# First layer of a hybrid decoder trunk: part of GpSimd's elementwise work is given to VectorE, and the whole program is put in a new order

## The chip, the core and the metric

The kernel runs on one core of a Trainium2 chip. The metric is the device time of that core in microseconds (us). In the profile TensorE is PE (its weight load is PEld), VectorE is DVE, ScalarE is ACT, GpSimd is POOL and SyncE is SP.

## The reference, cut to what matters

Two decoder layers on 512 tokens of width 1024, all in float32. The change touches the first half of the first layer: one input projection, whose columns feed a pooling mixer, an indexer that picks 128 keys for each query, and attention over the picked keys with a partial rotary embedding.

```
h = rmsnorm(x, ln_mix[0]);  p = h @ w_in_ab
u_pool, q, k, v, qi, ki, wi = columns of p
q, k, qi, ki = partial_rope(...)            # ki after its own rmsnorm
y_a = pool_mixer(u_pool)                    # 4 groups, causal windows 2, 4, 8, 16
s_idx = sum_h relu(qi_h . ki) * wi_h;  sel = top_k(s_idx, 128)      # causal
y_b = softmax(q . k[sel] / 8) @ v[sel]      # 4 blocks of 128 queries
x = x + [y_a, y_b] @ w_out_ab
x = x + swiglu(rmsnorm(x));  then layer 1 (gated linear recurrence, swiglu) and a final rmsnorm
```

`partial_rope` turns pairs of the first 16 of each 64 columns: `x1*cos - x2*sin`, `x2*cos + x1*sin`.

## The kernel before

Activations lie transposed, 128 channels by 512 tokens. Each fp32 operand of a projection is kept as a high part and a low part, and each product is three matmuls: high by high (`BH,wh`), low of the activation by high of the weight (`BL,wh`), and high by low of the weight (`BH,wl`). A weight unit of up to 512 columns arrives by DMA in `raw`, ScalarE rounds it to `wh` (a ring of 6 buffers), and a subtraction on VectorE or GpSimd makes `wl` (`split`, lines 490 to 497). Which engine subtracts is set by `lo_eng[0]`, a function of the running number u of the unit.

Work of the first layer in the order in which it is written: units 0 to 5 project the indexer's queries (two slabs), 6 and 7 its key, 8 and 9 the attention's key, 10 and 11 its value, 12 to 19 four slabs of queries, 20 to 27 the four groups of the pooling mixer. `rope` is called eight times (two indexer queries, the indexer's key, the attention's key, four slabs of queries): a shuffle of rows on VectorE, a product with the cosine on VectorE, a product with the sine, and a sum. The mixer adds shifted copies of a page on GpSimd (1, 2, 3 and 4 additions for the four groups). `topk` finds, for query blocks 3, 2 and 1, the threshold of the 128 largest scores by 16 rounds of MAX and MATCH_REPLACE on VectorE (512, 384 and 256 keys wide), and ends with one comparison that makes a bf16 mask; TensorE adds that mask to the scores by a matmul with the identity (`bk<-pa,idb`). Units 28 to 35 are the mixer's output projection (`w_oa`, all low parts on GpSimd); its results are added to `xT` on VectorE, and the two PSUM banks that it uses come free by these additions.

The order in which each engine executes is not the order of the code. `Plan` records every operation with its dependences, gives each an estimated duration, and runs a list scheduler forward and backward six times; then for each row (seed, sigma, a, w) of the table `MOVES` it disturbs the priorities of the operations that start between a and a+w (in ns of its own estimate) by random numbers, plans three times more, and keeps the order with the least estimated end. The instructions are then issued in that order from one line, so nearly every row of the profile says L414 (`getattr(self.real[o.eng], o.call)`), and instructions are told apart by tiles. Each engine executes its own list strictly in that order.

Names: `bk` PSUM banks, `pa` and `pg` pages of 128x512 in SBUF, `sm` small tiles, `BH`/`BL` the high and low parts of the activation (later also of the mixer's and the attention's output), `xT` the residual stream, `trib`/`idb` bf16 tiles of the causal mask and the identity.

Of the kernel before, what the change touches and what calls it, by code (L numbers as in the profile page):

```python
# [40 lines left out]
ITERS = 6  # L41

MOVES = (
# [20 lines left out]
)  # L64
PAGES = 38
RPAGES = 20
# [351 lines left out]
def trunk(ctx: ExitStack, tc: tile.TileContext, xt, xp, pos, vecs, ident, dup, tri, lmask, invc, select,  # L418
          w_ab, w_kw, w_pool, w_oa, w_ob, w_c, w_oc, w_gu, w_dn, w_dq, out):
    nc = Plan(tc)  # L420
# [3 lines left out]
    def new(shape, dt, name):  # L424
        t = cp.tile(shape, dt, name=name)
        return t[tuple(slice(None) for _ in shape)]
# [60 lines left out]
    lo_eng = [lambda u: nc.vector]  # L487
# [21 lines left out]
    def units(src, sizes, cols=P):  # L509
        t = load(src)  # L510
        off = 0
        for s in sizes:
            yield split(t[:, off:off + s * cols], cols)
            off += s * cols
# [159 lines left out]
    class Stage:  # L674
# [12 lines left out]
        def next(self):  # L687
            n = 1 + 2 * (self.n % 2)
            self.n += 1
            return self.b[0], self.b[n], self.b[n + 1]  # L690
# [152 lines left out]
    def std(srcs, ah, al):  # L843

        ps = main.get()
        us = [(src, s) for src, s in srcs]
        n, tot = 0, sum(len(k) for _, s in us for k in s)
        for src, s in us:
            for u, ks in zip(units(src, [len(k) for k in s]), s):
                mm3(ps, u, ah, al, ks, n == 0, n + len(ks) == tot)  # L850
                n += len(ks)
        return ps
# [4 lines left out]
    def layer0(br):  # L857
# [3 lines left out]
        trib = new([P, H2], BF16, "trib")  # L861
        upm = new([P, P], I32, "upm")
        neg = new([P, P], F32, "neg")
        lo_eng[0] = lambda u: nc.gpsimd if u % 4 < 3 else nc.vector


        nc.sync.dma_start(vec, vecs)
# [7 lines left out]
        ps = side.get()  # L875
# [4 lines left out]
        for j in range(KD):  # L880
# [4 lines left out]
            if j in (0, 1, 4):  # L885
                k0, k1 = {0: (0, 1), 1: (1, 4), 4: (4, 8)}[j]
                for q in range(2):
                    u = next(units(w_ab[10 + q][:, P * k0:P * k1], [k1 - k0]))
# [56 lines left out]
        for src, dst in ((CE, Ct), (SE, St)):  # L945
            ps = side.get()
# [12 lines left out]
        pages.put(acc)  # L959
        nc.vector.tensor_mul(r2, r_, r_)  # L960

        def rope(dst, src, c, s, slow=False):
            sh = pages.get()
            nc.vector.stream_shuffle(sh, src, SH)
            nc.vector.tensor_mul(dst, src, c)
            nc.gpsimd.tensor_mul(sh, sh, s)
            (nc.gpsimd if slow else nc.vector).tensor_add(dst, dst, sh)
            pages.put(sh)


# [4 lines left out]
        main.put(kps)  # L975
        qi = [pages.get() for _ in range(2)]
        rope(qi[0], pq[0], Ct, St)
        main.put(pq[0])
        ss = col_sums([ksq], 64)
# [16 lines left out]
        side.put(rkp)  # L996
        ki = pages.get()
        rope(ki, kin, Ct, St)
        rope(qi[1], pq[1], Ct, St)
        main.put(pq[1])  # L1000
        rp = bcast(r_)
        R, RC, RS = pages.get(), pages.get(), pages.get()
# [36 lines left out]
        def scores(at):  # L1039
            for b, w in ((3, 2), (2, 9), (1, 9)):  # L1040
                if w == at:
                    x = index(b)
                    sc[b] = x, topk(b, x)
# [5 lines left out]
        ps = std([(w_ab[8], two8)], xh, xl)  # L1049
# [4 lines left out]
        ps = std([(w_ab[9], two8)], xh, xl)  # L1054
# [11 lines left out]
        qT = []  # L1066
        for j in range(4):
            scores(3 + j)
            ps = std([(w_ab[4 + j], two8)], xh, xl)
            qT.append(pages.get())  # L1070
            rope(qT[j], ps, RC, RS, True)
            main.put(ps)

        def attend(b, bias, ops):
# [74 lines left out]
        for g in range(2):  # L1149
            for x, y in zip(khl, kd2[2 * g:]):  # L1150
                ps = side.get()
# [4 lines left out]
        for j in range(4):  # L1156
# [7 lines left out]
            ps = side.get()  # L1164
# [49 lines left out]
        for z in range(2):  # L1214
            ts = slice(z * H2, z * H2 + H2)
            for n, (m, u) in enumerate(held):
                ps = main.get()
# [319 lines left out]

    r0, r1, r2 = Bridge(V_FFN), Bridge(V_MIX + 8), Bridge(V_FFN + 8)
    layer0(r0)
    pages.free = [b for b in pages.free if all(b is not x for x in early_pg)]  # L1540
    ffn(0, r1)
# [98 lines left out]
```

## Time and profile before

| | us |
|---|---|
| median of 3 runs | 1209.56 (1207.65 to 1212.93) |
| the profiled execution | 1210.61 |
| its span, first to last instruction | 1208.8 |
| PE busy | 1171.1 (97%) |
| DVE busy | 977.6 (81%) |
| ACT busy | 754.6 (62%) |
| POOL busy | 231.3 (19%) |

The profiled execution is 1.8 us longer than its span, and 1.05 us above the median. PE's busy share counts pipelined matmuls, so a short wait of PE shows as idle time only where it is longer than what is still in flight.

### The profile page before, as it was taken

How to read it: one execution, taken by the hardware profiler on the slowest of the kernel's cores; microseconds unless marked ns; L12 is line 12 of the kernel's file. 1: busy time of each engine (PE TensorE's matmuls, PEld its weight loads, DVE VectorE, ACT ScalarE, POOL GpSimd, SP SyncE). 2: the span in 40 equal slices, each digit the busy share in tenths (PEclk: the TensorE clock that was granted, in tenths of full speed). 3: DMA queues.
4: the chain of work that ended last, by engine and by line, in shares of the span. 5: the costliest groups of instructions: out<-in, count | busy, mean ns of one | idle time of the engine just before them, and what ended most of it. 6: DMA issues, size and time to landing. Idle time of an engine off the chain costs nothing.

```text
span 1208.8 us, 23135 instructions
## 1 busy us (share of the span) xinstructions
PE 1171.1 (97%) x8563; PEld 1074.0 (89%) x8563; DVE 977.6 (81%) x2116; ACT 754.6 (62%) x1753; POOL 231.3 (19%) x209
## 2 busy tenths in 40 slices
PE   8997999999999999998999999999999999999996
PEld 6775658999999988998899999988999999998996
DVE  7799965997777794777999999976987777894676
ACT  6336974766666672655777767744776666672563
POOL 4465112121111000113322222111221111000111
PEclk9998999999999999998999999999999999999999
DMA  9212023589867534576675444316489876634652
GB/s 330 85 53 70 18 53 87 170 232 235 230 173 208 129 115 139 135 169 175 209 180 138 125 121 109 100 57 158 159 235 233 227 185 174 161 103 123 150 151 70
DMA packets 72369, 180.60 MB, mean 149 GB/s; under 512 B 6144, under 2 KB 20544, under 8 KB 72256
## 3 DMA queue, kind: packets, MB, share of 16 engines
q1 hardware_dynamic: 51584, 141.37, 36.0%
q0 software_dynamic: 20672, 37.75, 18.7%
q8 instruction: 67, 1.10, 0.4%
q14 instruction: 46, 0.38, 0.1%
HBM read 177.00 MB, written 2.10 MB: 148 GB/s over the span
## 4 chain that ended last, share of the span: by engine, by line
PE 71%; DVE 7%; DMA 5%; ACT 4%; issue 2%; POOL 1%; DVEq 0%; POOLq 0%; ACTq 0%
PE bk L414 71%; DVE wl L414 3%; DMA raw<-in_w_dq 2%; DMA raw<-in_w_gu 2%; DVE pg L414 2%; ACT wh L414 2%; ACT pg L414 1%; POOL pg L414 1%; DVE raw L414 1%; DVE BL L414 1%; ACT bk L414 1%; DVE xT L414 1%; DMA raw<-in_w_c 0%; DVE pa L414 0%; DVE sm L414 0%
## 5 line engine op out<-in xcount | busy, mean ns | idle before, releaser
L414 PE MATMUL bk<-BH,wh 128*128 128x256 f32 (+1 forms) x2088 | 587.0, 297 | 9.9 <-ACT bk L414 3.9
L414 PE MATMUL bk<-BL,wh 128*128 128x256 f32 (+1 forms) x2088 | 588.5, 294 | 3.4 <-DVE BL L414 2.1
L414 PE MATMUL bk<-BH,wl 128*128 128x256 f32 (+1 forms) x2088 | 579.1, 294 | 1.7 <-DVE wl L414 1.3
L414 ACT ACTIVATE wh<-raw 128x512 fp32r<-128x512 f32 (+2 forms) x644 | 378.8, 603 | 280.2 <-PE bk L414 236.6
L414 DVE TENSOR_TENSOR wl<-raw,wh 128x512 fp32r<-128x512 f32 (+1 forms) x609 | 399.1, 672 | 111.5 <-ACT wh L414 92.6
L414 PEld LDWEIGHTS bk<-BH,wh 128*128 128x128 f32 x2088 | 389.8, 192 | 25.7 <-ACT bk L414 7.3
L414 PEld LDWEIGHTS bk<-BL,wh 128*128 128x128 f32 x2088 | 393.5, 192 | 13.3 <-DVE BL L414 3.5
L414 PEld LDWEIGHTS bk<-BH,wl 128*128 128x128 f32 x2088 | 388.6, 192 | 10.8 <-DVE wl L414 2.2
L414 PE MATMUL bk<-pr,wh 128*128 128x256 f32 (+1 forms) x784 | 190.4, 331 | 0.5 <-ACT wh L414 0.5
L414 PEld LDWEIGHTS bk<-pr,wh 128*128 128x128 f32 x784 | 132.0, 189 | 15.3 <-ACT wh L414 0.7
L414 PE MATMUL bk<-pr,wl 128*128 128x256 f32 (+1 forms) x392 | 129.0, 332 | 0.6 <-DVE wl L414 0.6
L414 DVE TENSOR_TENSOR raw<-raw 128x512 f32<-128x512 f32 (+1 forms) x152 | 102.7, 680 | 10.7 <-DMA raw<-in_w_gu 5.5
L414 POOL DMA_DIRECT2D raw<-in_w_gu x44 | 48.0, 1090 | 328.5 <-DMA raw<-in_w_gu 124.3
L414 DVE TENSOR_TENSOR pg<-pg,pg 128x256 f32<-128x256 f32 (+2 forms) x203 | 99.2, 499 | 9.0 <-ACT pg L414 4.5
L414 ACT COPY pg<-bk 128x256 f32<-128x256 f32 (+6 forms) x212 | 76.2, 365 | 29.4 <-PE bk L414 26.4
L414 ACT COPY bk<-bk 128x256 f32<-128x256 f32 x222 | 77.5, 362 | 23.9 <-PE bk L414 23.5
L414 PEld LDWEIGHTS bk<-pr,wl 128*128 128x128 f32 x392 | 73.5, 188 | 8.1 <-DVE wl L414 1.1
L414 PE MATMUL bk<-pg,pg 128*128 128x128 f32 (+3 forms) x578 | 66.7, 259 | 2.7 <-issue 1.6
L414 POOL TENSOR_TENSOR wl<-raw,wh 128x512 fp32r<-128x512 f32 (+3 forms) x35 | 45.8, 1313 | 93.6 <-ACT wh L414 85.7
L414 PEld LDWEIGHTS bk<-pg,pg 128*128 128x128 f32 (+3 forms) x578 | 55.3, 167 | 9.0 <-issue 2.8
L414 POOL TENSOR_TENSOR pg<-pg,pg 128x256 f32<-128x256 f32 (+1 forms) x36 | 39.3, 1094 | 114.3 <-ACT pg L414 62.5
L414 POOL DMA_DIRECT2D raw<-in_w_dq x16 | 17.5, 1096 | 223.2 <-DVE wl L414 164.1
(167 smaller groups left out, 1062.8 us busy)
## 6 DMA issues: line engine op xcount, KB each, us to landing
raw<-in_w_gu SPq DMA_DIRECT2D x44, 768.0 KB, 5.6
raw<-in_w_gu SPq DMA_DIRECT2D x64, 512.0 KB, 5.0
raw<-in_w_gu POOLq DMA_DIRECT2D x44, 512.0 KB, 6.6
raw<-in_w_c SPq DMA_DIRECT2D x16, 768.0 KB, 5.3
raw<-in_w_c SPq DMA_DIRECT2D x21, 512.0 KB, 3.9
raw<-in_w_dq SPq DMA_DIRECT2D x16, 576.0 KB, 5.7
raw<-in_w_c POOLq DMA_DIRECT2D x16, 512.0 KB, 6.9
raw<-in_w_dn SPq DMA_DIRECT2D x16, 448.0 KB, 3.4
```

Of the source, the lines that this page charges most:

```text
L414: getattr(self.real[o.eng], o.call)(*map(_real, o.args), **{k: _real(v) for k, v in o.kw.items()})
```

## The change

Three edits in `layer0`, and another table `MOVES` (75 rows in place of 60):

- units 0 to 27: GpSimd subtracts for odd u alone (14 of 28), in place of u % 4 < 3 (21 of 28). VectorE gets units 0, 2, 4, ..., and gives 3, 7, 11, ... to GpSimd;
- the product with the sine of all eight rotations goes from GpSimd to VectorE;
- the sum of the four rotations of the query slabs goes from GpSimd to VectorE.

```
@@ -41,26 +41,30 @@
 MOVES = (
-    (353236198, 1000, 372111, 20000), (664781755, 200, 1057486, 200000), (787263731, 2000, 158073, 40000),
...
+    (288545018, 1000, 132344, 40000), (1047664193, 50, 817488, 80000), (4522707, 2000, 934044, 40000),
...
@@ -861,7 +865,7 @@
-        lo_eng[0] = lambda u: nc.gpsimd if u % 4 < 3 else nc.vector
+        lo_eng[0] = lambda u: nc.gpsimd if u % 2 else nc.vector
@@ -959,12 +963,12 @@
-        def rope(dst, src, c, s, slow=False):
+        def rope(dst, src, c, s):
             sh = pages.get()
             nc.vector.stream_shuffle(sh, src, SH)
             nc.vector.tensor_mul(dst, src, c)
-            nc.gpsimd.tensor_mul(sh, sh, s)
-            (nc.gpsimd if slow else nc.vector).tensor_add(dst, dst, sh)
+            nc.vector.tensor_mul(sh, sh, s)
+            nc.vector.tensor_add(dst, dst, sh)
             pages.put(sh)
@@ -1068,7 +1072,7 @@
-            rope(qT[j], ps, RC, RS, True)
+            rope(qT[j], ps, RC, RS)
```

Since the planner starts from other operations and other random numbers, the lists of all engines differ from end to end. Three places follow.

POOL, in the middle of the input projections. `wl` rows are low parts; the others are products and sums of rotations. Before:

```order
L414 TENSOR_TENSOR pa6_111<-pa6_111,pg14_139 128x512
L414 TENSOR_TENSOR pa10_115<-pa10_115,pg14_139 128x512
L414 TENSOR_TENSOR pa16_121<-pa16_121,pa13_118 128x512
L414 TENSOR_TENSOR wl4_94<-raw2_83,wh4_88 128x512
L414 TENSOR_TENSOR wl5_95<-raw2_83,wh5_89 128x512
L414 TENSOR_TENSOR wl0_90<-raw0_81,wh0_84 128x512
L414 TENSOR_TENSOR pa9_114<-pa9_114,pg14_139 128x512
L414 TENSOR_TENSOR pg7_132<-pg7_132,pa13_118 128x512
L414 TENSOR_TENSOR pg6_131<-pg6_131,pg7_132 128x512
L414 TENSOR_TENSOR wl2_92<-raw1_82,wh2_86 128x512
L414 TENSOR_TENSOR wl3_93<-raw1_82,wh3_87 128x512
L414 TENSOR_TENSOR pg9_134<-pg9_134,pa13_118 128x512
```

The same place on POOL with the change, up to the first addition of the mixer (`128x511`):

```order
L418 TENSOR_TENSOR wl5_95<-raw2_83,wh5_89 128x512
L418 TENSOR_TENSOR wl1_91<-raw0_81,wh1_85 128x512
L418 TENSOR_TENSOR wl3_93<-raw1_82,wh3_87 128x512
L418 TENSOR_TENSOR wl5_95<-raw2_83,wh5_89 128x512
L418 TENSOR_TENSOR wl1_91<-raw0_81,wh1_85 128x512
L418 TENSOR_TENSOR wl3_93<-raw1_82,wh3_87 128x512
L418 TENSOR_TENSOR wl5_95<-raw2_83,wh5_89 128x512
L418 TENSOR_TENSOR wl1_91<-raw0_81,wh1_85 128x512
L418 TENSOR_TENSOR wl3_93<-raw1_82,wh3_87 128x512
L418 TENSOR_TENSOR pg9_134<-pg5_130 128x511
```

The rotations have left POOL, and every second low part; POOL's whole list has 194 rows in place of 213.

DVE, from the first MAX of query block 3 on (`pa18`, `pa19` hold the 512-wide scores). Before:

```order
L414 MAX sm2_98<-pa18_123 128x8
L414 TENSOR_TENSOR pg8_133<-bk0_143,pa12_117 128x512
L414 MATCH_REPLACE pa19_124<-sm2_98,pa18_123 128x512
L414 MAX sm3_99<-pa19_124 128x8
L414 MATCH_REPLACE pa18_123<-sm3_99,pa19_124 128x512
L414 MAX sm4_100<-pa18_123 128x8
L414 MATCH_REPLACE pa19_124<-sm4_100,pa18_123 128x512
L414 STREAM_SHUFFLE pg11_136<-bk1_144 128x512
L414 MAX sm5_101<-pa19_124 128x8
L414 TENSOR_TENSOR pg10_135<-bk1_144,pa12_117 128x512
L414 MATCH_REPLACE pa18_123<-sm5_101,pa19_124 128x512
L414 TENSOR_TENSOR wl5_95<-raw2_83,wh5_89 128x512
```

The same place on DVE with the change:

```order
L418 MAX sm2_98<-pa18_123 128x8
L418 STREAM_SHUFFLE pg7_132<-bk2_145 128x512
L418 MATCH_REPLACE pa19_124<-sm2_98,pa18_123 128x512
L418 TENSOR_TENSOR pg6_131<-bk2_145,pa12_117 128x512
L418 MAX sm3_99<-pa19_124 128x8
L418 TENSOR_TENSOR pg7_132<-pg7_132,pa13_118 128x512
L418 MATCH_REPLACE pa18_123<-sm3_99,pa19_124 128x512
L418 TENSOR_TENSOR pg6_131<-pg6_131,pg7_132 128x512
L418 MAX sm4_100<-pa18_123 128x8
L418 TENSOR_TENSOR wl2_92<-raw1_82,wh2_86 128x512
L418 MATCH_REPLACE pa19_124<-sm4_100,pa18_123 128x512
L418 TENSOR_TENSOR pg8_133<-bk0_143,pa12_117 128x512
```

Between two rounds of the selection there now stand rotations and low parts. From the first MAX to the comparison that ends block 3, DVE's list has 113 rows in place of 94, and it holds 4 MAX of block 2 in place of 6.

PE, at the end of the input projections (`bk1<-..wl3` is the last of them): the mixer's four small products (`pa6` holds the four pool weights, a pair of rows each), the doubling of the attention's key (`pa4`), and the first unit of `w_oa` (`wh4_88`, `wl4_94`). Before:

```order
L414 MATMUL bk1_144<-BH3_76,wl3_93 128x512
L414 MATMUL bk6_149<-pg7_132,pa6_111 128x256 x2
L414 MATMUL bk7_150<-pg2_127,pa6_111 128x256 x2
L414 MATMUL bk5_148<-pg13_138,pa6_111 128x256 x2
L414 MATMUL bk7_150<-BH0_73,pa4_109 128x512
L414 MATMUL bk7_150<-BL0_77,pa4_109 128x512
L414 MATMUL bk6_149<-pg17_142,pa6_111 128x256 x2
L414 MATMUL bk5_148<-BL0_77,pa4_109 128x512
L414 MATMUL bk7_150<-BL2_79,pa4_109 128x512
```

The same place on PE with the change:

```order
L418 MATMUL bk7_150<-BL2_79,pa4_109 128x512
L418 MATMUL bk2_145<-pa0_105,BH2_75 128x256
L418 MATMUL bk7_150<-BH0_73,wh4_88 128x512
L418 MATMUL bk7_150<-BL0_77,wh4_88 128x512
L418 MATMUL bk7_150<-BH0_73,wl4_94 128x512
L418 MATMUL bk5_148<-pg13_138,pa6_111 128x256 x2
L418 MATMUL bk7_150<-BH1_74,wh4_88 128x512
L418 MATMUL bk7_150<-BL1_78,wh4_88 128x512
L418 MATMUL bk6_149<-pg17_142,pa6_111 128x256 x2
L418 MATMUL bk7_150<-BH1_74,wl4_94 128x512
```

Five matmuls of `w_oa` now stand ahead of the last mixer product (`pg17`), where before there was none; up to the first matmul with the mask of block 3 there are 41 of them in place of 35.

## Rows read from the trace of the kernel before

**Rows 1.** Windows by stage: busy us (x instructions) of each engine, granted clock, DMA share, GB/s.
```profile
0.00:60.00 60.00, 53.87 (x259) 39.87 (x260) 45.98 (x104) 30.98 (x61) 28.74 (x28) 0.97 0.60 208
60.00:125.00 65.00, 57.59 (x240) 42.73 (x238) 62.50 (x126) 31.47 (x66) 38.23 (x30) 0.95 0.19 59
100.00:125.00 25.00, 17.59 (x68) 11.74 (x66) 23.45 (x46) 16.78 (x36) 11.44 (x10) 0.86 0.07 22
...
125.00:210.00 85.00, 84.20 (x427) 57.10 (x427) 60.97 (x195) 58.45 (x155) 12.01 (x11) 1.00 0.21 51
540.00:810.00 270.00, 262.91 (x2199) 250.15 (x2198) 246.98 (x586) 187.62 (x489) 64.53 (x57) 0.98 0.50 136
810.00:1208.00 398.00, 384.38 (x2908) 367.20 (x2906) 299.83 (x602) 237.02 (x525) 48.02 (x47) 0.99 0.61 162
```
**Rows 2.** Waits of PE from 100 to 130 us: us in total, times, longest.
```profile
PE bk L414 <- DVE pg L414: 4.7, 3, 2.9
...
PE bk L414 <- DVE xT L414: 1.1, 1, 1.1
```
**Rows 3.** Chain of work that ended last, first layer: start, us, what.
```profile
109.46 0.76 DVE pg L414 x2
...
124.89 0.68 DVE xT L414
...
125.61 69.72 PE bk L414 x314
```
**Rows 4.** Groups on POOL by shape, 0 to 60 us, then 60 to 125: busy, mean ns.
```profile
L414 POOL TENSOR_TENSOR wl<-raw,wh 128x512 fp32r<-128x512 f32 x11 | 15.5, 1419 | 16.2 <-ACT wh L414 14.8 <-DMA xT<-in_xp 1.4
...
L414 POOL TENSOR_TENSOR pg<-pg,pg 128x512 f32<-128x512 f32 x3 | 3.9, 1294 | 0.2
```
**Rows 5.** Groups on DVE by shape, 300 to 500 us, where POOL hardly works.
```profile
L414 DVE TENSOR_TENSOR wl<-raw,wh 128x512 fp32r<-128x512 f32 x101 | 67.8, 687 | 28.6 <-ACT wh L414 20.6 <-PE bk L414 6.9
```
**Rows 6.** Groups on DVE by shape, 0 to 60 us.
```profile
L414 DVE TENSOR_TENSOR pg<-pg,pg 128x512 f32<-128x512 f32 x7 | 8.4, 1206 | 0.1
...
L414 DVE SCALAR_TENSOR_TENSOR sm<-sm 128x4 f32<-128x4 f32 x12 | 3.5, 295 | 0.2
L414 DVE TENSOR_TENSOR wl<-raw,wh 128x512 fp32r<-128x512 f32 x3 | 3.1, 1040 | 0.0
L414 DVE TENSOR_TENSOR pa<-pa,pa 128x512 f32<-128x512 f32 x3 | 3.1, 1036 | 0.0
...
L414 DVE TENSOR_TENSOR sm<-sm 128x4 f32<-128x4 f32 x6 | 0.9, 157 | 0.1
```
**Rows 7.** Groups on DVE by shape, 60 to 125 us.
```profile
L414 DVE TENSOR_TENSOR pg<-bk,pa 128x512 f32<-128x512 f32 x6 | 4.1, 676 | 0.5 <-PE bk L414 0.5
...
L414 DVE MAX8 sm<-pa 128x8 f32<-128x384 f32 x7 | 3.9, 560 | 0.2
L414 DVE MATCH_REPLACE8 pa<-sm,pa 128x384 f32<-128x384 f32 x6 | 3.3, 546 | 0.0
L414 DVE TENSOR_TENSOR wl<-raw,wh 128x512 fp32r<-128x512 f32 x2 | 3.0, 1514 | 0.0
...
L414 DVE SCALAR_TENSOR_TENSOR pa<-pg,tok,pa 128x512 f32<-128x512 f32 x2 | 2.3, 1168 | 0.2
...
L414 DVE TENSOR_TENSOR pg<-pg,pg 128x16 f32<-128x16 f32 x7 | 2.2, 328 | 0.0
```
**Rows 8.** Timeline of POOL, then of DVE: start, us, instruction.
```profile
70.56 1.30 POOL L414 TENSOR_TENSOR pg<-pg,pg 128x512 f32<-128x512 f32 x1
...
70.86 1.55 DVE L414 TENSOR_TENSOR wl<-raw,wh 128x512 fp32r<-128x512 f32 x1
...
122.80 1.50 DVE L414 TENSOR_SCALAR pa<-pa 128x512 bf16<-128x512 f32 x1
```
**Rows 9.** Timeline of PE: start, us, instruction, idle before.
```profile
105.75 1.13 PE L414 MATMUL bk<-pg,pa 128*128 128x256 f32 x4 [2.90 <-DVE pg L414]
...
128.65 0.38 PE L414 MATMUL bk<-pa,idb 128*128 128x512 bf16 x1
```

42 rows, old and new, of the table MOVES are left out of this document.

## The prediction

> **What bounds the kernel now.** I read first the windows by stage, to see which engine is full where. PE is busy for almost every microsecond from 125 us to the end; the only stretch in which it stands still for long is 100 to 125 us, where it works 17.6 of 25 us, and its clock is granted at 0.86 on the mean [rows 1]. So the kernel's time is PE's work, which the change leaves as it is, plus what PE waits, and the first layer's share of those waits lies at the end of the input projections. Next the waits of PE there: 4.7 us on pages that DVE makes (the mixer's pooled pages, the longest 2.9 us at 105.75) and 1.1 us on an addition to `xT` that frees a bank [rows 2, 9]. The chain that ended last says the same: it runs through DVE from 109.46 to 125.57 us without a break, and then through 314 matmuls of PE for 69.7 us [rows 3]. DVE is the engine that decides when PE gets going again. It is busy for 62.5 of the 65 us from 60 to 125, and POOL for 38.2 of them [rows 1]. That is the stretch into which the change puts more work for DVE.
>
> How the two engines disturb each other is the third thing to read. A low part of 512 columns takes DVE 0.687 us where POOL is idle [rows 5]. In the first layer the same instruction takes 1.04 us on the mean before 60 us, and 1.51 us after it; the additions `pg<-pg,pg` take 1.21 us [rows 6, 7]. The timeline shows why: the low part that starts at 70.86 takes 1.55 us, and POOL's addition of 1.30 us, begun at 70.56, ends at 71.86; DVE's 0.69 us fit in behind that end [rows 8]. Not every DVE instruction waits so: a product with one operand in a PSUM bank stays at 0.676 us, and MAX on 384 keys at 0.560 [rows 7]. So DVE pays for POOL's work only in instructions with both operands in SBUF, and in some small ones.
>
> **The change, part by part.** *What is taken from POOL.* Seven low parts on balance (14 leave, 7 come: six of 512 columns and one of 128), and 12 products and sums of rotations. Undisturbed, one of 512 columns takes 1.294 us [rows 4], so this is 18 x 1.294 + 0.6 = 23.9 us of POOL's time. POOL itself is not full: it waits for ScalarE's `wh` for 16.2 us ahead of 60 us [rows 4], and is busy for 38.2 of the next 65 [rows 1]. So this gain counts only through DVE.
>
> *What is put on DVE.* 18 instructions of 0.687 us [rows 5] and a small one of some 0.3: 12.7 us. By place: ahead of 60 us (units 0 to 18) five of the wide low parts, the small one and six of the rotations' instructions, 7.9 us; behind it one and six, 4.8 us.
>
> *What DVE gets back.* Its waits for POOL. Ahead of 60 us the three groups of 512-wide instructions hold 7 x 0.52 + 3 x 0.35 + 3 x 0.35 = 5.7 us over the 0.687 of an undisturbed one, and the twelve `sm` instructions 12 x 0.14 = 1.7 us over 0.157 [rows 6]: 7.4 us, over POOL's 21 tensor instructions (its 28 [rows 1] less the 7 memsets at the head of its list) 0.35 us each. From 60 to 125 us: 2 x 0.83 (low parts), 2 x 0.48, 7 x 0.17 [rows 7] and 0.8 for the comparison at 122.80, which takes 1.50 us [rows 8]: 4.6 us over 30 POOL instructions, 0.15 each. Instructions that stand alone in those views are not in these sums, so I take 0.45 and 0.22. POOL loses 12 instructions ahead of 60 us and 7 behind: 5.4 + 1.5 = 6.9 us back.
>
> *What it pays anew.* The 19 moved instructions have both operands in SBUF and so wait themselves. The 13 of their kind ahead of 60 us waited 0.44 us each; with 9 POOL instructions in place of 21 I take 0.44 x 9 / 21 = 0.19, and 12 x 0.19 = 2.3 us; behind 60 us 0.2 x 7 = 1.4 us. Balance for DVE: 12.7 - 6.9 + 3.7 = +9.5 us. Bounds: if nothing comes back, 16.4; if each of POOL's 23.9 us had held DVE up, 12.7 - 23.9 = -11.2. The rows stand far nearer to the upper bound, since POOL was busy for 67 us ahead of 125 us [rows 1] and the excess found on DVE is 12.
>
> *What covers it.* First, two rounds of the selection for block 2 now stand behind the comparison of block 3, 2 x (0.56 + 0.55) = 2.2 us [rows 7]. Second, DVE stood idle for 14.0 of the first 60 us [rows 1], waiting for data; the 7.9 - 5.4 + 2.3 = 4.8 us that it gains there on balance go half into these holes, I take 2.4. That leaves the mask of block 3 later by 9.5 - 2.2 - 2.4 = 4.9 us. In the trace it was ready at 124.30 (the comparison's end) and PE took it up at 128.65 [rows 8, 9]: 4.35 us of cover. So it is late by some 0.5 us, not by 9. What lies behind it on DVE, the rest of the selection for blocks 2 and 1, has room: DVE is idle for 24 of the 85 us from 125 to 210 [rows 1]. What is late next is the mixer's last products, queued on DVE behind the added work: some 3 us later, by the work added ahead of 105 us less what is absorbed. Against this, PE's list now has five matmuls of `w_oa` ahead of the last mixer product, at 57.6 us / 240 = 0.24 us each [rows 1], so 1.2 us of its wait are filled. The two results overlap, since the same wait of PE is paid once: I take +1.5 us, between 0 (all covered) and +4.9 (nothing filled).
>
> A part of the change has no price in these rows: the new order of the other stages. PE stands idle for 7.1 us from 540 to 810 and 13.6 us from 810 on [rows 1]; in those stages the order can give or take some of that. I take 0.
>
> Sum: the profiled execution's 1210.6 (span 1208.8 and 1.8 around it) + 1.5 = 1212.1. That execution lies 1.05 us above the median of the three runs; on the median's footing it is 1211.1. I forecast 1211.5, which no measurement of this kernel tells from no change: the runs shown spread over 0.4%, so I call all within 0.5% (6 us) the same.
>
> **Two rules.** The Trainium skill, "SBUF — State Buffer", section "Who interferes with whom", says that a VectorE instruction with two SBUF inputs and a GpSimd instruction that reads SBUF exclude each other for the whole instruction, whichever came first. The trace agrees in the 1.55 us against 0.687 and in the PSUM product's 0.676. Read alone it favours the change, since each moved instruction frees more of the shared port than it takes; that is the first rival. The same page of the Trainium skill, section "Summary: rules for kernel authors", advises that of such a pair the work off the critical path should be the one that is blocked; by that the change goes the wrong way, as DVE is on the path here, and its time is the second rival's.
>
> **The rivals.** *DVE gains.* If POOL's hold on DVE is really larger than the groups show, DVE ends the selection earlier, the mixer's pages come in time, and PE's idle 7.4 us of 100 to 125 [rows 1] shrink. At most all go: 1210.6 - 7.4 = 1203.2. For it: DVE's waits on `wl` of 0.83 us each behind 60 us [rows 7], where only two of them were tried. Against it: the excess found is 12 us, spread over instructions of which many only shift idle time.
>
> *The cover is gone (slower).* Place: the comparison of block 3. If DVE gets nothing back and absorbs nothing, it ends 12.7 - 2.2 = 10.5 us later, 6.1 past the cover: 1216.7, and with the new waits of 3.7 us 1220.4. It decides as soon as the mask is ready after 128.65. For it: DVE's 96% in that stretch. Against it: 14 us of holes ahead of it.
>
> *The edits do nothing, the order does all.* The lists of all engines are new to the end. A quarter of PE's 20.7 us of idle time behind 540 us, either way: 1205.4 or 1215.8.
>
> **How the numbers follow.** Chances: the forecast 0.50, DVE gains 0.15, the cover gone 0.20, the order alone 0.15 (half each way). Within 0.5% of 1209.6 means 1203.5 to 1215.6. Faster than that: most of the first rival, little of the rest, 0.18. Slower: most of the second, half of the order's bad half, a tail of the forecast, 0.25. The same: 0.57. The range runs from the first rival's end to short of the second's far end, 1203 to 1219; some 0.2 lies outside.
>
> **What would show it.** POOL ahead of 125 us should have 19 instructions fewer and about 24 us less; DVE some 9 us more, with `wl` nearer to 0.8 than to 1.2 us. The mask of block 3 should be ready at about 129 us, and PE's idle time of 100 to 130 us should stay at 7 to 9 us; the chain should still enter PE there, at 125 to 129 us. I am wrong if the mask comes before 124 and PE's wait falls under 4 us (first rival), if it comes past 131 us (second), or if the first 210 us end at the same place and the difference lies behind 540 us (third).

## The result, and the profile after

The changed kernel takes 1220.2 us (median of 6 runs, 1216.1 to 1222.2), the kernel before 1209.15 us beside it (6 runs). The ratio is 1.008 with a 95% interval of 1.0064 to 1.0096: 9.7 us slower, beyond the 0.5% that the prediction called measurable. By the ratio that is 1218.8 us, barely inside the range of 1203 to 1219; the median lies 1.2 us above it. The ratios, here and below, leave out four disturbed runs of 1872 to 6343 us, and they differ by up to 0.2% from the quotients of the medians (1.0091 here). The profiled execution of the changed kernel took 1221.29 us, its span is 1219.5 us, 10.7 more than before.

The first line of the profile's page, busy time of each engine and instructions, changed kernel:

```profile
PE 1180.7 (97%) x8562; PEld 1082.1 (89%) x8563; DVE 978.6 (80%) x2135; ACT 756.1 (62%) x1753; POOL 207.3 (17%) x190
```

POOL has lost 19 instructions and 24.0 us, DVE has 19 more, yet is busy for only 1.0 us more. Windows by stage, changed kernel (busy us and instructions of PE, PEld, DVE, ACT, POOL, then granted clock, DMA share, GB/s), to be laid beside [rows 1]:

```profile
0.00:60.00 60.00, 54.47 (x238) 39.61 (x238) 42.52 (x110) 29.01 (x58) 12.76 (x16) 0.89 0.57 201
60.00:125.00 65.00, 60.22 (x243) 45.71 (x243) 63.60 (x115) 28.81 (x60) 29.93 (x22) 0.95 0.20 65
100.00:125.00 25.00, 20.37 (x74) 14.81 (x73) 23.92 (x41) 16.34 (x34) 14.91 (x12) 0.86 0.14 43
125.00:210.00 85.00, 85.00 (x420) 56.09 (x420) 66.72 (x213) 60.71 (x160) 12.43 (x10) 1.00 0.21 50
540.00:810.00 270.00, 259.44 (x2187) 249.33 (x2186) 242.51 (x584) 189.41 (x488) 62.50 (x57) 0.99 0.53 140
```

Two things stand out. The place that the prediction watched, 100 to 125 us, has got better: PE is busy for 20.37 us in place of 17.59. And ahead of 60 us the clock is granted at 0.89 in place of 0.97, and PE has issued 238 matmuls in place of 259. To see where time goes, I compared when PE starts its n-th matmul in both traces (one record of the changed kernel's 8563 is missing, which is nothing at this scale); starts are from the span's start:

```
n-th matmul of PE      200   250   400   500   950  2950  3700  4200  5700  5950  7700  8450
before, us            46.8  57.0  93.1 126.2 214.3 475.8 577.9 640.6 818.1 857.0  1070  1185
changed - before, us  +4.6  +6.2  +5.1  +2.9  +2.7  +5.1  +9.8  +7.0  +7.8 +11.6 +13.8 +10.3
```

PE is 6 us late by 57 us, has 3 of them back by 126 us, loses another 5 by 578 us of which 3 come back by 640, loses 4 around 850 us, and gets 3 back at the end. The first loss is in PE's timeline (start, us, instruction, idle before), changed kernel:

```profile
25.46 0.95 PE L418 MATMUL bk<-ones,pg 128*128 128x1 f32 x8
29.61 0.33 PE L418 MATMUL bk<-idn,pg 128*128 128x128 f32 x1 [3.20 <-DVE pg L418]
29.69 0.48 PE L418 MATMUL bk<-BH,wh 128*128 128x512 f32 x1
...
43.44 0.63 PE L418 MATMUL bk<-BH,wh 128*128 128x512 f32 x1
43.87 0.51 PE L418 MATMUL bk<-BL,wh 128*128 128x512 f32 x1
44.22 0.39 PE L418 MATMUL bk<-BH,wl 128*128 128x512 f32 x1
44.45 0.40 PE L418 MATMUL bk<-BH,wh 128*128 128x512 f32 x1
```

PE stands for 3.20 us before the first transpose of the rotation angles (`bk<-idn,pg`), which DVE computes in small steps. Up to 43.9 us matmuls of 512 columns start 0.43 us apart, and 0.23 us apart from 44.2: the 1.2 GHz level, then 2.4. The windows of 25 to 50 us say the same, first of the kernel before, then of the changed one (columns as above):

```profile
25.00:50.00 25.00, 23.03 (x111) 17.80 (x110) 20.49 (x67) 9.55 (x20) 9.98 (x8) 0.93 0.41 142
```

```profile
25.00:50.00 25.00, 21.80 (x84) 16.54 (x83) 15.51 (x56) 6.26 (x14) 2.58 (x2) 0.73 0.34 122
```

A granted share of 0.73 over 25 us means that 27% of the clock's time, 6.8 us, was not granted; before it was 0.07 x 25 = 1.8 us. So in these two executions 5.0 us of the 6.2 are the clock's, and the remainder is about the longer wait: 3.20 us against the 1.56 of the kernel before, whose line is

```profile
31.30 1.22 PE L414 MATMUL bk<-pg,pg 64*128 64x512 f32 x2 [1.56 <-issue]
```

### The profile page after: what moved, and what is told of

The parts are those of the page before. It is cut to its first block, busy times and chain, and to the rows that moved or that the text cites. A ratio compares the mean times of both kernels' runs of the same rounds, so it can differ in the third digit from the quotient of the medians.

```text
span 1219.5 us, 23140 instructions
## 1 busy us (share of the span) xinstructions
PE 1180.7 (97%) x8562; PEld 1082.1 (89%) x8563; DVE 978.6 (80%) x2135; ACT 756.1 (62%) x1753; POOL 207.3 (17%) x190
## 4 chain that ended last, share of the span: by engine, by line
PE 80%; DVE 9%; DMA 5%; ACT 3%; issue 2%; POOL 1%; SPq 0%; DVEq 0%; ACTq 0%; POOLq 0%
PE bk L418 80%; DVE pg L418 4%; DMA raw<-in_w_gu 3%; DVE wl L418 2%; DMA raw<-in_w_dq 1%; ACT wh L418 1%; DVE pa L418 1%; ACT pg L418 1%; DVE BL L418 1%; DVE sm L418 1%; POOL pg L418 1%; DVE xT L418 0%; ACT BH L418 0%; DMA raw<-in_w_c 0%; DMA xT<-in_xt 0%
## 5 line engine op out<-in xcount | busy, mean ns | idle before, releaser
L418 DVE TENSOR_TENSOR wl<-raw,wh 128x512 fp32r<-128x512 f32 (+2 forms) x616 | 398.1, 661 | 129.5 <-ACT wh L418 116.2
L418 POOL TENSOR_TENSOR wl<-raw,wh 128x512 fp32r<-128x512 f32 (+3 forms) x28 | 37.8, 1350 | 125.2 <-ACT wh L418 106.9
L418 POOL TENSOR_TENSOR pg<-pg,pg 128x256 f32<-128x256 f32 (+1 forms) x32 | 35.4, 1106 | 125.6 <-ACT pg L418 52.3
```

Source lines behind the costliest of these rows:

```text
L418: getattr(self.real[o.eng], o.call)(*map(_real, o.args), **{k: _real(v) for k, v in o.kw.items()})
```

## The experiments

The planner's search can't be steered, so each kernel below has its order written out as a list and issues from it; the edit is the same in all, and only the list and the three edits of the change differ:

```
-        (the planner's search over MOVES)
+        d = np.frombuffer(zlib.decompress(base64.b85decode("".join(LISTED))), np.int16)
+        order = np.cumsum(d.astype(np.int64)).tolist()
```

Both kernels record the same 12754 operations with the same dependences; 33 of them are on another engine. `old` and `new` are the two lists. What was measured, each against the kernel before on the same chip (us is the ratio times the 1209.5 of the kernel before; the medians are of this run and of the kernel before beside it):

```
run                      ratio   95% interval       us   medians        what it is
e3_edits_old_order       1.0017  1.0003..1.0031   +2.1   1212.8/1209.8  edits, old list
e4_order_alone           1.0082  1.0059..1.0106   +9.9   1221.8/1209.8  no edits, new list
e1_first_layer_alone     1.0042  1.0025..1.0058   +5.1   1215.2/1209.8  edits, new first layer, old rest
e2_rest_alone            1.0142  1.0119..1.0164  +17.2   1228.7/1209.8  no edits, old first layer, new rest
f1_first_60us_old        1.0038  1.0020..1.0057   +4.6   1214.9/1209.7  edits, old to 60 us, then new
f4_old_to_400us          1.0048  1.0030..1.0067   +5.8   1217.3/1209.7  edits, old to 400 us, then new
f2_old_to_700us          1.0035  1.0018..1.0052   +4.2   1214.8/1209.7  edits, old to 700 us, then new
f3_new_tail_only         0.9984  0.9968..1.0001   -1.9   1209.5/1209.7  no edits, old to 1050 us, then new
h1_pe_33_places          1.0027  1.0010..1.0045   +3.3   1214.2/1209.2  edits, new list, 33 places of PE old
h2_old_one_stall         1.0056  1.0035..1.0078   +6.8   1215.6/1209.2  no edits, old list, 4 transposes ahead
h3_old_mended            1.0011  0.9994..1.0028   +1.3   1211.3/1209.2  no edits, old list, one pair back
h4_old_mended_new_tail   0.9984  0.9966..1.0001   -1.9   1208.7/1209.2  h3 with the new tail
```

### The edits without the order, and the order without the edits

```
 e3: order = old                 (all three edits)
 e4: order = new                 (none of the edits)
```

> All of the edits (the 33 operations change their engine, the low parts are cut in halves) in the list of the kernel before throughout, so that nothing is reordered. My forecast's sum (about 10 us more on VectorE ahead of the mask, most of it covered): 1209 to 1213. Its rival, the cover is gone (VectorE's 10 to 16 us come out at the mask that block 3 waits for): 1216 to 1221. If the edits themselves cost what the changed kernel loses, this one is as slow as it, 1220.

> None of the edits (GpSimd makes what it made in the kernel before), in the changed kernel's list throughout, first layer and all. If the order of the list is most of the loss: 1216 to 1220. If the edits carry it: 1209 to 1212. Theory 1 as for the first two runs (some 3 us in the first layer, of which the edits may be part, and 8 us behind it by the order): 1217 to 1220.

The edits alone cost 2.1 us (0.4 to 3.7): near the forecast's +1.5, and not "the cover is gone". The order alone costs 9.9 us, as much as the changed kernel, so in the new list the edits make no difference that can be seen (1.0082 without, 1.0080 with). Thus the order is the cause. It was drawn for operations on their new engines, and without the edits it need not lose at the same places: in the trace of `e4` PE is 10.8 us late at the 250th matmul, in that of the changed kernel 6.2. Neither part of the edits was tried alone, since each would lie below what such an interval tells.

How the edits come to cost so little is in the trace of `e3_edits_old_order`: windows of the first two stages, then the first line of its page.

```profile
0.00:60.00 60.00, 55.13 (x266) 40.24 (x267) 46.33 (x118) 31.36 (x61) 13.54 (x17) 1.00 0.60 209
60.00:125.00 65.00, 58.33 (x233) 43.30 (x232) 61.99 (x134) 30.94 (x66) 27.55 (x22) 0.89 0.17 57
```

```profile
PE 1173.1 (97%) x8563; PEld 1075.9 (89%) x8563; DVE 976.1 (81%) x2135; ACT 754.3 (62%) x1753; POOL 205.1 (17%) x190
```

With 19 instructions more, DVE is busy for 976.1 us, where it was 977.6 before; in the traces of `f3`, `h2`, `h3` and `h4`, which have no edits and the old list for most of the program, it is 976.2 to 976.8. So it got back all of the 12.7 us that were put on it.

### Which part of the order

```
 e1: order = old, places of the first layer's operations filled in new's order   (edits)
 e2: order = old, places of all later operations filled in new's order           (none)
```

> The change's edits, with the changed kernel's order of the first layer (operations up to the end of the first mixer half); everything behind it in the order of the kernel before. Theory 1 (the time is lost place by place: in the two traces the n-th matmul of the changed kernel is late by 2.9 us at the end of the first layer, and the other 8 us or so come at four places far behind it, where only the order differs): about 1212, that is 2 to 4 us over the kernel before. Theory 2 (the first layer's delay is the cause, and all that comes behind is its echo): 1218 to 1221, as the changed kernel. Theory 3 (the first layer costs nothing by itself): within 1 us of the kernel before, 1209 to 1210.

> The kernel before with none of the edits and its own order of the first layer; everything behind the first layer in the changed kernel's order, in which no instruction differs but by its place. Theory 1 (the order of the later stages costs by itself): 1216 to 1219, 7 to 9 us over the kernel before. Theory 2 (the later losses are the echo of the first layer's delay): 1208 to 1211, no change.

`e1` took 5.1 us more, a little above theory 1's figure and far under theory 2's: its lateness is 4.3 us at the 500th matmul and 4.3 us at the 7700th, so nothing echoes. `e2` missed every expectation. The dependences moved over a hundred operations at its cut, PE lost another 9 us between the 700th and the 1200th matmul (175 to 258 us of its trace), where the changed kernel loses nothing, and so it tells nothing of the later order. The next cuts were made where both lists have done the same to within some ten operations, and need no repair:

```
+k = place behind the n-th operation of TensorE in old     (n = 250, 2350, 4500, 7100)
+order = old[:k] + [i for i in new if i not in old[:k]]
```

> The changed kernel (all edits) with its list, but the list's first 250 TensorE operations, some 60 us, and all that the list of the kernel before has ahead of the 250th, stand in the old order. In the changed kernel's trace TensorE waits 3.2 us at 29.6 us and then has the half clock for 13.7 us (3.4 before), and is 6 us late by 60 us, of which 3 come back by 130 us. Theory (the first 60 us of the new order cost this, by their own waits and the low clock behind them): no half clock longer than 7 us ahead of 60 us, and 1213 to 1217 in place of the changed kernel's 1220. Rival (the delay is made good later anyway, or the edits make it in any order): 1219 to 1221.

> All edits, the old list up to the 2350th TensorE operation (some 400 us, in the midst of the first feed-forward half), from there the changed kernel's list. Against the run with the old list to 700 us it adds the seam of feed-forward half and layer 1, 510 to 600 us, where TensorE waits 6.0 us for ScalarE's pages in the changed kernel and 1.3 before, and half of that came back by 615 us. Theory (each seam costs by its own order): 2 to 3 us over that run, 1214 to 1217. Rival (only the first layer costs): the same as that run.

> All edits, the old list up to the 4500th TensorE operation (some 700 us, in the midst of layer 1), from there the changed kernel's list. Theory (the seam between layer 1 and its feed-forward half, 845 to 865 us, costs 4 us by its own order, through a wait of 1.3 us and 6.8 us of half clock behind it, and the end of the new list gives 2 to 3 back): edits 2 + 4 - 2.5, 1211.5 to 1215, with a new stretch of half clock near 850 us. Rival (that loss is an echo of what came before): 1209 to 1211.5 and no half clock there.

> The kernel before without any edit, with its own list up to the 7100th TensorE operation (some 1050 us), and the changed kernel's list from there to the end. In the changed kernel's trace the matmuls come 13.8 us late at 1070 us and the end only 10.7 us late, so the new end of the list should be 1.5 to 3 us the faster. Theory: 1206.5 to 1208.5. Rival (it only makes good what it was late by): 1209.5 to 1210.5, the same as before.

`f1` came out as its theory had it: with the old order for 60 us alone, 5.1 of the 9.7 us are gone (the difference of two ratios, so give or take 3). The later seams are less clear. Between `f4` and `f2` lies the seam at 510 to 600 us. PE's waits there (us in total, times, longest), in `f4`, which has the new order there, then in `f2`, which has the old:

```profile
PE bk L548 <- ACT pg L548: 5.3, 4, 3.1
```

```profile
PE bk L546 <- ACT bk L546: 1.8, 4, 0.7
PE bk L546 <- ACT pg L546: 1.5, 2, 0.8
```

The waits for ScalarE's pages go with the list, but the time differs by 1.6 us, less than the intervals tell. The time of `f2` lies in its theory's range, but the stretch of low clock near 850 us that the theory rests on is not there. Windows of 850 to 870 us, of the changed kernel, then of `f1`, whose list from 60 us on is the same:

```profile
850.00:870.00 20.00, 18.28 (x124) 17.68 (x124) 15.38 (x37) 11.97 (x29) 4.78 (x6) 0.83 0.41 109
```

```profile
850.00:870.00 20.00, 19.68 (x158) 18.90 (x158) 19.98 (x47) 15.81 (x39) 6.65 (x8) 1.00 0.48 155
```

The same list has the low clock there in one execution and the full clock in the other; `f2` has 1.00 too, `f4` has 0.91. So the 4 us at 850 us in the profile of the changed kernel are not a property of its order alone. What set them off there stays open. `f3` has 1.9 us less by the ratio, as its theory had it, but its interval just holds no change.

### Which instructions: 33 places of one engine

> The changed kernel in all but 33 places of TensorE's own list (its operations 117 to 149, 26 to 35 us), which hold the same operations in the order that they have in the kernel before: the four transposes of the rotation angles (bk from idn,pg) come behind 13 projections of which every operand is long made, in place of ahead of them. Every other engine's list is that of the changed kernel. Theory (these transposes stall TensorE for 3.2 us with ready work behind them, and the half clock of 13.7 us follows that stall): no wait over 1.6 us near 30 us, a half clock of 7 us or less ahead of 60 us, and 1214 to 1217 in place of 1220. Rival (TensorE is only late with what VectorE hands it, whatever its own order): 1219 to 1221.

The rows of PE's list, changed kernel (-) and `h1` (+); the projections are `bk3<-..`, their operands were made long before:

```
 bk5_148<-ones_63,pg2_127 128x1 x4
-bk6_149<-idn_62,pg11_136 128x128
 bk3_146<-BH0_73,wh2_86 128x512
 bk3_146<-BL0_77,wh2_86 128x512
-bk6_149<-idn_62,pg11_136 128x128 x3
-bk5_148<-pg15_140,pg0_125 128x512
-bk7_150<-idn_62,pg12_137 128x128 x4
-bk6_149<-ones_63,pg16_141 128x1 x4
 bk3_146<-BH0_73,wl2_92 128x512
...
 bk3_146<-BH2_75,wh3_87 128x512
+bk6_149<-idn_62,pg11_136 128x128 x4
+bk7_150<-idn_62,pg12_137 128x128 x4
```

> The kernel before without any edit, in which only the four transposes of the rotation angles (bk from idn,pg) are moved ahead on TensorE's list, in front of the 14 projections that they follow, as in the changed kernel. VectorE hands over their operand near 31 us, so TensorE should stand from 28 to 31 us. Theory (a stall there of 3 us and the low clock behind it is most of what the changed kernel loses ahead of 60 us): a half clock of some 10 to 14 us near 32 us and 1212.5 to 1216. Rival (the stall is made good by the slack behind it): 1209 to 1211.

In the kernel before (-) and `h2` (+):

```
 bk5_148<-ones_63,pg2_127 128x1 x4
+bk6_149<-idn_62,pg11_136 128x128 x4
 bk3_146<-BH0_73,wh2_86 128x512
...
 bk3_146<-BH2_75,wh3_87 128x512
-bk6_149<-idn_62,pg11_136 128x128 x4
 bk7_150<-idn_62,pg12_137 128x128 x4
```

`h1` gives back 6.4 of the 9.7 us (1.0080 to 1.0027, give or take 3), and `h2`, which has no edit of the change and four operations in another place, loses 6.8 (4.2 to 9.4). PE's timeline of `h1`, then of `h2`:

```profile
30.06 1.09 PE L547 MATMUL bk<-pg,pg 64*128 64x512 f32 x2 [1.63 <-ACT pg L547]
32.61 1.04 PE L547 MATMUL bk<-idn,pg 128*128 128x128 f32 x8
```

```profile
32.39 1.12 PE L545 MATMUL bk<-idn,pg 128*128 128x128 f32 x4 [4.49 <-DVE pg L545]
```

In `h1` the transposes come when their operand is there, and the longest wait is 1.63 us. In `h2` PE stands for 4.49 us, with 13 ready projections behind the transposes (the fourteenth operation passed is the pair of products), is 3.8 us late at the 250th matmul, and 4.1 at the 2950th: there is no slack that makes it good; the span of this execution is 1213.7 us, 4.9 more than that of the kernel before. The low clock came otherwise than expected. Windows of 25 to 50 us of `h1`, then of `h2`:

```profile
25.00:50.00 25.00, 22.70 (x106) 17.79 (x105) 20.24 (x67) 6.84 (x16) 2.66 (x3) 0.86 0.40 146
```

```profile
25.00:50.00 25.00, 20.08 (x92) 14.94 (x91) 17.19 (x61) 7.64 (x15) 7.60 (x7) 0.86 0.39 142
```

0.86 is 3.5 us not granted in both, after a wait of 1.63 us and after one of 4.49; the changed kernel lost 6.8 after one of 3.20. So the place of these operations is shown to cost the time, from both sides, but how long the clock stays low behind the stall doesn't follow from the wait's length.

One trace has the clock of one execution. The time that the clock withheld is known for every execution that the ratios count, as its span times (1 - its granted clock). Means, less those of the kernel before (15.4 to 15.6 us withheld, in all three sets of its executions), each give or take about 2 us (`h3` follows below):

```
run                    withheld, us   remainder of the span, us
changed kernel             +4.1          +5.0
e1_first_layer_alone       +4.2          +0.5
f1_first_60us_old           0.0          +4.6
f2_old_to_700us            +1.5          +3.3
e3_edits_old_order         +2.5          -0.1
e4_order_alone             +5.3          +5.4
h1_pe_33_places            +1.7          +2.2
h2_old_one_stall           +4.2          +2.2
h3_old_mended              +2.4          -1.4
```

So the changed kernel's loss has two halves, and the order without the edits (`e4`) has both. `e1`, which has the new order in the first layer alone (and the edits), shows the clock's half and hardly anything else; `f1`, which has the old order to 60 us, shows none of it and nearly all of the remainder, much of which is still there when the new order begins at 700 us (`f2`). Which operations cost it there was not tried. Two rows don't fit neatly: `h1` gives back 2.9 us of the remainder, more than `f1` does, and in `e3` the clock withheld 2.5 us more although the order is the old one.

### A better version

> The kernel before without any edit, in which one operation is moved on TensorE's list: the pair of products bk from pg,pg (64x512), for which TensorE waits 1.6 us at 31.3 us in the kernel before with ready projections behind it, goes behind the next six projections. Theory (wait and the 3.4 us of half clock behind it go): 1.5 to 3 us less, 1206.5 to 1208.5. Rival (the half clock comes anyway, and the wait was in work that is made good): 1209 to 1210.

> The mended kernel before of the last run (one operation moved on TensorE's list near 31 us) with the changed kernel's list from its 7100th TensorE operation (some 1050 us) to the end, which was 1.9 us less than the kernel before when it was run alone. If both count: 1204.5 to 1207. If only the new end of the list does: 1207 to 1208.5. If neither: 1209 to 1210.

```
 bk3_146<-BH1_74,wh2_86 128x512
-bk5_148<-pg15_140,pg0_125 128x512
 bk3_146<-BL1_78,wh2_86 128x512
...
 bk3_146<-BH2_75,wh3_87 128x512
+bk5_148<-pg15_140,pg0_125 128x512
 bk6_149<-idn_62,pg11_136 128x128 x4
```

The wait went, the time did not (+1.3, the interval holds no change). `h3` is the last run of the table above. PE's timeline of `h3`, where the pair of products now starts without a wait, and its window of 25 to 50 us:

```profile
31.91 1.12 PE L546 MATMUL bk<-pg,pg 64*128 64x512 f32 x2
32.96 1.09 PE L546 MATMUL bk<-idn,pg 128*128 128x128 f32 x8
```

```profile
25.00:50.00 25.00, 24.95 (x123) 19.48 (x122) 19.75 (x64) 10.57 (x23) 10.19 (x8) 0.93 0.43 151
```

PE has no hole left in these 25 us and the clock is still granted at 0.93, as before the move: the expectation that it would rise with the wait gone is wrong. Over all executions the remainder fell by 1.4 us, about the wait, and the clock withheld 2.4 us more; where it did so was not looked for. The new tail gave 0.9984 again in `h4`. Two runs with that ratio speak for a small gain, but each interval reaches 1.0001, and the medians lie only 0.2 and 0.6 us under the kernel before: no version here is shown to beat it.

## Why the prediction came out too low

The step that failed is "a part of the change has no price in these rows: the new order of the other stages ... I take 0". The order alone is 9.9 us. The rival that named the order ended at 1215.8, because I took a quarter of PE's idle time behind 540 us as its measure; the piece that was found, 6.4 us by `h1`, lay at 26 to 35 us, in the stage for which I had costed the edits alone. The old trace held the wait's part of the price: DVE's last step of the angles ended near 31 us, PE's projections were ready from 28 us, and the new list put the transposes in front of them. DVE's line, then PE's, kernel before:

```profile
30.96 0.18 DVE L414 TENSOR_SCALAR pg<-pg 128x32 f32<-128x32 f32 x1
```

```profile
27.90 0.48 PE L414 MATMUL bk<-BH,wh 128*128 128x512 f32 x1
```

The clock's part could not be read there. I read the new order at the three places where the edits are, and not where PE's small matmuls stand among the projections. The chance of 0.25 for slower was too low for that reason. That 1218.8 lies inside the range is luck: the upper end was set by the rival in which the cover is gone, and `e3` refutes that rival.

Point by point:

- *POOL*: right. Ahead of 125 us it has 38 instructions for 58, and 42.7 us for 67.0 [rows 1].
- *DVE's balance of +9.5 us*: mis-sized. In the old order it is -1.5 to 0 over the whole program, since DVE got back some 13 us on balance and not 6.9 less 3.7. My sums counted waits only in groups where a mean stood out. The low parts in the changed kernel, DVE's groups by shape of 0 to 60 us, then of 60 to 125 us, against 1040 and 1514 ns in [rows 6, 7]:

```profile
L418 DVE TENSOR_TENSOR wl<-raw,wh 128x512 fp32r<-128x512 f32 x7 | 4.8, 679 | 3.7 <-ACT wh L418 3.7
```

```profile
L418 DVE TENSOR_TENSOR wl<-raw,wh 128x512 fp32r<-128x512 f32 x4 | 2.7, 677 | 0.0
```

They wait for POOL no more; in `e3` those ahead of 60 us still take 820 ns. In the new order the return is smaller: 978.6 us with the edits, 970.8 in `e4_order_alone` without, so +7.8. (A reading of mine was off without weight in the sum: of POOL's 16.2 us in [rows 4], 14.8 were for `wh`.)

- *The mask of block 3 at about 129 us*: it came past 131, the sign that I had named for the second rival. DVE's timeline, then PE's, changed kernel:

```profile
132.69 0.40 DVE L418 TENSOR_SCALAR pa<-pa 128x512 bf16<-128x512 f32 x1
```

```profile
133.47 0.38 PE L418 MATMUL bk<-pa,idb 128*128 128x512 bf16 x1
```

But the sign was a bad one. PE is busy for 85.00 of 85 us behind 125 us, and between the 500th and the 950th matmul it loses nothing: its new list has other work ahead of the mask. The cover is what stands ahead in PE's list, not a fixed 4.35 us. In `e3`, with the old list, the mask was ready at 123.4 and taken at 128.0, as before.

- *PE idle for 7 to 9 us of 100 to 130, the chain entering PE at 125 to 129*: wrong. Waits of PE from 100 to 130 us, and the chain of work that ended last, changed kernel:

```profile
PE bk L418 <- DVE BL L418: 2.3, 1, 2.3
PE bk L418 <- ACT pa L418: 1.4, 2, 0.7
...
PE bk L418 <- ACT BL L418: 0.3, 1, 0.3
```

```profile
29.61 38.08 PE bk L418 x149
...
106.92 2.32 DVE BL L418 x2
...
113.67 94.58 PE bk L418 x440
```

PE waits 4.7 us in place of 7.9 (before, 4.7 + 1.1 as in [rows 2], and 1.8 and 0.3 on `pa` and `BL`), and the chain enters it at 113.67 in place of 125.61 [rows 3]. That is the 3 us that come back by 126 us. The chain also shows the new bound: PE from 29.61 us on, where the stall ends.

- *The sum*: the edits' +1.5 us was measured as +2.1 (0.4 to 3.7), but the agreement is luck. DVE's balance was taken much too high, and the cover that was to hide it was not needed: in the trace of `e3` PE is 0.6 us early at the 500th matmul, and over its executions the remainder is the same as before (-0.1) and the clock withheld 2.5 us more. Why it did so isn't known.

Of the 9.7 us the runs trace 6.4 to 33 places of PE's list, give or take 3. `e1` and `f1`, 5.1 and 4.6, part the loss into the first layer and what lies behind 60 us; they add up to 9.7, though both have the edits. The part behind 60 us isn't traced to operations.

## What to carry to other kernels

When a change draws a new order, price the order first. Go down the list of the engine that bounds the kernel, find each instruction that has moved ahead of work that is ready, and look up in the old trace when its operand is made; placing four transposes too early stalled a full engine for 3.2 and 4.5 us, and putting them right or wrong moved the end by 6.4 and 6.8 us. And test an edit in the old order: it took one kernel to part a change of 2 us from a reshuffle of 10. Where the differences are that small, split the time by the granted clock of all executions, not of one.

## What the runs showed of the hardware

The low clock ahead of 60 us differs between executions of the same instructions. `e3`, `f1`, `f2` and `f4` have the same list up to PE's 250th operation, near 57 us, and the same edits. From 25 to 50 us the clock was granted at 1.00 in `e3` and at 0.86 in the other three, which is 3.5 us, after a wait of the same length. Windows of `e3`, then of `f4`; then PE's wait in `e3`, and in `f1`:

```profile
25.00:50.00 25.00, 22.83 (x121) 18.19 (x120) 20.18 (x71) 10.63 (x22) 3.82 (x3) 1.00 0.46 160
```

```profile
25.00:50.00 25.00, 22.83 (x103) 17.73 (x102) 19.27 (x70) 8.85 (x17) 3.49 (x3) 0.86 0.39 141
```

```profile
30.40 1.09 PE L546 MATMUL bk<-pg,pg 64*128 64x512 f32 x2 [1.58 <-issue]
```

```profile
31.35 1.09 PE L547 MATMUL bk<-pg,pg 64*128 64x512 f32 x2 [1.53 <-issue]
```

PE is busy for 22.83 us in both and gets 121 matmuls done in one, 103 in the other. The Trainium skill, "TensorE: Matmul & The Clock Gate", Part 1, says of the start of a kernel that the number of matmuls run at the low level varies from run to run; these rows show a variation of that kind 30 us into the program. So a loss that one profile shows with the clock low, as that at 850 us here, is to be seen in a second execution before it is explained.

That GpSimd's work costs VectorE so much was the other surprise. In the same order, 26.2 us taken from POOL (231.3 to 205.1) gave DVE some 13 us back: it took on 12.7 us of work, and its busy time, 976.1 us, is no longer than without the edits (976.2 to 977.6).
